# An encoder's first layer: norm factor r applied where the projections leave PSUM, raw X transposed

## The chip, the cores and the metric

The kernel runs on one core of a Trainium2 chip. The metric is the time of one launch on the device in microseconds (us). Beside it stand profiles: one execution recorded by the hardware profiler. PE is TensorE (its weight loads are a row PEld), DVE is VectorE, ACT is ScalarE, POOL is GpSimd, SP is SyncE, which issues most DMAs. Each engine works through its own instructions in order and waits on semaphores of the others.

## The reference, cut to what matters

A bidirectional encoder over 1024 tokens of width 1024, in float32, with two layers. Layer 0 mixes tokens by two-dimensional neighbourhood attention, layer 1 by grouped-query attention with rotary positions. The diff touches only layer 0's head:

```python
def rms_norm(x, g):
    y = xf * lax.rsqrt(jnp.mean(xf * xf, axis=-1, keepdims=True) + NORM_EPS)
    return (y * g.astype(jnp.float32)).astype(x.dtype)

h = rms_norm(x, norm_g[0])
q, k, v, gate = jnp.split(h @ w_in, 4, axis=-1)      # w_in: 1024 x 4096, 16 heads of 64
sc = einsum('bhqd,bhqnd->bhqn', q, k[window]) * scale + bias
o = einsum('bhqn,bhqnd->bhqd', softmax(sc), v[window])
y = (o * silu(gate)) @ w_out
```

The norm factor r = 1/sqrt(mean(x*x) + eps) is one number for each token; the gain g is one number for each of the 1024 features. So h @ w is r * ((x * g) @ w), row by row.

## The kernel before, in words

Tokens are handled in 8 tiles of 128. Every large matmul is made of three: both operands are split into a high part in the fp32r format and a low part, the remainder (split3, L302: high x high, high x low, low x high).

**The transposed input.** HTh and HTl hold the normalised, transposed input, high and low, for 8 tiles x 8 chunks of 128 features. to_ht (L420 to L427) makes them: PE transposes four 128x128 chunks into one PSUM bank (L425), ACT copies the bank into HTh (L426), DVE subtracts that copy from the bank into HTl (L427); two such halves make a tile.

**The weights.** The class Weights holds a queue of weight units. stage (L200) issues the DMA of a 512 KB unit from SP into one of a few slots; pump lets ACT make the high part wh (L215), and settle lets DVE make the low part wl (L216). A slot is free again when wl is done.

**The start of mixer_a (L697 to L786)** is a sequence written by hand. Per tile t: load X[t] (L706); square (L709, ACT's Square with a sum along the row); newton (L713 and L312 to L322: r by an integer first guess and three steps, 13 small DVE instructions on 1, 2 or 4 columns), which weave spreads between other pieces of work; scale (tiles 0, 1, 2, 4, 6: one DVE instruction X*r*g, L725; tiles 3, 5, 7: ACT times r, L727, then POOL times g, L728); then ht(t), the transposes of the scaled X. After that come vs[t][0] and vs[t][1], the two halves of the V projection of tile t for the first four heads (24 matmuls of 256 columns in all). Its result leaves PSUM by ACT into V's high part (L579) and by DVE into its low part (L580). PE's order is vs[t][0], transposes of tile t+1, vs[t][1].

**Beside it** SP loads the mask and the position bias (8 DMAs into U), expands U to U2 (16 DMAs, L778), and table (L618 to L627) loads a head's bias (L621) and subtracts it from the mask on POOL (L624).

**Then attention.** For head 0, qk_items runs the q and k projection: matmuls with 512 tokens as columns and 128 rows of features (64 of q, 64 of k). qk_evac (L583 to L609) copies the bank on ACT into a tile raw (L593), and from it ACT and DVE make the split q and k. gate_items (L516) does the same for the gate: ACT copies the bank to G (L520), ACT's tanh reads G (L521). For each head, scores (f_S), exponentials (f_E), transposes of the probabilities (f_T) and the product with V (f_AV) are interleaved with the projection of the following head and the gates, by a planner that fills PE's time by costs written beside each piece; V for the heads 4 to 15 is projected in the same way, through the same v_items.

PSUM's eight banks in this stage: pd (projections, 2), psS (scores, 2), psT (transposes, 2), psO (outputs, 2).

Of the kernel before, what the change touches and what calls it, by code (L numbers as in the profile page):

```python
# [11 lines left out]
F32 = mybir.dt.float32  # L12
# [3 lines left out]
AF = mybir.ActivationFunctionType  # L16
ALU = mybir.AluOpType
# [4 lines left out]
NT = 8  # L22
KC = 8
D = 1024
HD = 64
NH = 16
EPS = 1e-6
# [9 lines left out]
DT = (5, 2)  # L37
FIN = (4, 4)
HOLD = 2
DP = 1  # L40
KD, KS = 3, 4
QD = (2, 5, 8)
# [40 lines left out]
def lay_out(inp):  # L83
    g = {k: np.asarray(v) for k, v in inp.items()}
# [7 lines left out]
    aq, ak, av, ag = np.split(g["a_w_in"][0], 4, axis=1)  # L92
# [48 lines left out]
    def swap(v):  # L141
# [4 lines left out]
    return {  # L146
        "x": tokens(g["x"][0]), "wts": W, "rpb": rpb, "gains": gains, "hgains": hg,
        "mask": mask, "rope": np.stack([cosT, sinT], axis=1),
    }


@with_exitstack
def trunk(ctx, tc, x, wts, rpb, gains, hgains, mask, rope, out):
    nc = tc.nc
    sync, act, dve, pool, pe = nc.sync, nc.scalar, nc.vector, nc.gpsimd, nc.tensor

# [264 lines left out]
    def to_ht(pt, t, xn, cs=(0, 1)):  # L421
        for c in cs:
            ps = pt.tile([128, 4, 128], F32, name="t")
            for k in range(4):
                pe.transpose(ps[:, k], xn[:, (4 * c + k) * 128:(4 * c + k + 1) * 128], ident)  # L425
            act.activation(HTh[:, t, 4 * c:4 * c + 4], ps, AF.Copy)  # L426
            dve.tensor_tensor(HTl[:, t, 4 * c:4 * c + 4], ps, HTh[:, t, 4 * c:4 * c + 4], ALU.subtract)  # L427
# [124 lines left out]
    def mixer_a():  # L552
        with ExitStack() as es:
# [10 lines left out]
            def dalloc():  # L564
                return pd.tile([128, 512], F32, name="d")

            def valloc():
                return pd.tile([128, 512], F32, name="d")[:, :256]

            gg, ylive = {}, {}  # L570
# [3 lines left out]
            def v_items(qd, t):  # L574
                keys = [("av", qd, 0), ("av", qd, 1)]

                def evac(ps):
                    v = ps.rearrange("p (h d) -> p h d", h=4)
                    act.activation(V[:, t, :, 0:64], v, AF.Copy)  # L579
                    dve.tensor_tensor(V[:, t, :, 64:128], v, V[:, t, :, 0:64], ALU.subtract)  # L580
                return [d[0] for d in proj_N(keys, t, 256, valloc, evac, release=keys if t == NT - 1 else ())]

            def qk_evac(h, hf):  # L583
                def evac(ps):
                    if hf == 0:
                        QS[h] = qkp.tile([128, 1024], F32R, name="QS")
                        KA[h] = qkp.tile([128, 1024], F32R, name="KA")
                        KB[h] = qkp.tile([128, 1024], F32R, name="KB")
                    s = slice(hf * 512, (hf + 1) * 512)
                    lo, hi = slice(0, 64), slice(64, 128)  # L590
                    qs, ka, kb = QS[h], KA[h], KB[h]
                    raw = sb.tile([128, 512], F32, name="th", bufs=2)
                    act.activation(raw, ps, AF.Copy)  # L593
# [81 lines left out]
            def f_AV(h, kb):  # L675
# [3 lines left out]
                for hf in range(2):  # L679
# [12 lines left out]
                    if last:  # L692
                        fin = head_end(sb, h, hf, RS[h][:, 4 * hf:4 * hf + 4], OP[h][hf], ylive, 0, gg, talloc)
                        if fin:
                            later.add(FIN[0], fin)

            e2 = es.enter_context(ExitStack())  # L697
            ini = e2.enter_context(tc.tile_pool(name="ini", bufs=1))
            X = [ini.tile([128, D], F32, name=f"X{t}") for t in range(NT)]
            gt = ini.tile([128, D], F32, name="gain")  # L700
            junk = ini.tile([128, D], BF16, name="junk")
            stat = one.tile([128, 3, 8], F32, name="stat")
            wk = one.tile([128, 24], F32, name="wki")

            def load(t):
                sync.dma_start(X[t], x[t])  # L706

            def square(t):
                act.activation(junk, X[t], AF.Square, accum_out=stat[:, 0, t:t + 1])  # L709

            def newton(a, b):
                ms = stat[:, 1, a:b]
                return [lambda: dve.tensor_scalar(ms, stat[:, 0, a:b], 1.0 / D, EPS, op0=ALU.mult, op1=ALU.add)] \  # L713
                    + rsqrt_ops(stat[:, 2, a:b], ms, wk)

            def weave(ops, fs):
                per = -(-len(ops) // len(fs))
                for i, f in enumerate(fs):
                    for o in ops[i * per:(i + 1) * per]:
                        o()  # L720
                    f()

            def scale(t):
                if t % 2 == 0 or t == 1:
                    dve.scalar_tensor_tensor(X[t], X[t], stat[:, 2, t:t + 1], gt, op0=ALU.mult, op1=ALU.mult)  # L725
                else:
                    act.activation(X[t], X[t], AF.Copy, scale=stat[:, 2, t:t + 1])  # L727
                    pool.tensor_tensor(X[t], X[t], gt, ALU.mult)  # L728

            def ht(t):  # L730
                return [lambda c=c: to_ht(psT, t, X[t], (c,)) for c in range(2)]

            load(0)
            sync.dma_start(gt, bcast(gains, 0, D))
            load(1)
            WQ.stage(True)
            for t in range(2, NT):
                load(t)
            U = dram.tile([16, 8, 31, 24], F32, name="U")
            square(0)  # L740
            square(1)
            weave(newton(0, 1), [lambda: scale(0)])
            WQ.pump(True)
            WQ.pump(True)
            vs = [v_items(0, t) for t in range(NT)]
            weave(newton(1, 2), ht(0))
            scale(1)
            square(2)
            square(3)
            vs[0][0]()  # L750
            weave(newton(2, 4), ht(1))
            scale(2)
            scale(3)
            square(4)
            square(5)
            square(6)
            vs[0][1]()
            sync.dma_start(MK, mask)
            for c in range(8):
# [1 line left out]
            for t in range(1, NT):  # L761
                vs[t][0]()
                if t + 1 < NT:
                    weave(newton(4, 8) if t == 2 else [], ht(t + 1))
                if t == 1:
                    square(7)
                if t in (2, 3):
                    scale(2 * t)
                    scale(2 * t + 1)
                vs[t][1]()  # L770
                if t == 6:
                    table(0)
                WQ.pump(t > 2)
                if t == 3:
                    for r in range(16):
                        src = bass.AP(tensor=U.tensor, offset=U.offset + (15 - r) * 24,
                                      ap=[[5952, 16], [744, 8], [1, 384]])
                        sync.dma_start(U2[:, r * 8:(r + 1) * 8, :], src)  # L778
            e2.close()
            qkp = es.enter_context(tc.tile_pool(name="qkp", bufs=2))  # L780
            ptp = es.enter_context(tc.tile_pool(name="ptp", bufs=1))
# [22 lines left out]
            for h in range(NH):  # L804
# [24 lines left out]
                    dense += qk_items(h + 1)  # L829
                p = h // 2  # L830
                if h < 14:
                    dense += gate_items("ag", p, h % 2, dalloc, sb, gg)
                elif h == 14:
                    dense += gate_items("ag", 7, 0, dalloc, sb, gg) + gate_items("ag", 7, 1, dalloc, sb, gg)
# [454 lines left out]
    dense_phase(1)  # L1289


NAMES = ["x", "wts", "rpb", "gains", "hgains", "mask", "rope"]


# [13 lines left out]
```

## Time and profile before

| | before |
|---|---|
| median of 3 runs | 1585.03 us (1583.64 to 1585.88) |
| the profiled execution's own time | 1586.45 us |
| its span | 1584.7 us |
| mean granted clock of PE | 0.996 |
| busy share of the span: PE, DVE, ACT, POOL | 96%, 65%, 55%, 17% |

A timeline row reads: start in us, duration in us, engine, line of the kernel, operation, output<-inputs, their shapes, a count if several stand in the row, and in brackets how long the engine had been idle and what released it. A row of groups reads: line, engine, operation, names, shapes and count, then busy us in all and the mean ns of one, then the engine's idle time ahead of them and its releaser. A row of waits reads: who waited for whom, us in all, how often, the longest.

### The profile page before, as it was taken

What the parts mean: (1) busy time and instruction counts of PE and PEld (TensorE: products, weight loads), DVE (VectorE), ACT (ScalarE), POOL (GpSimd) and SP (SyncE); (2) the same over time, 40 slices, a digit from 0 to 9 for tenths busy, and PEclk for the clock granted to TensorE, in tenths of its full rate; (3) what the DMA queues carried; (4) which work ended last, traced back from release to release, by engine and by line L of the source; (5) the groups of instructions that cost most, each with busy time, mean ns of one, the idle gap of its engine ahead of it and who ended that gap; (6) DMA issues with size and microseconds to landing.
All of it is one profiled execution on the core that took longest, in us unless ns stands there. A gap on an engine that the chain in (4) does not pass through costs nothing.

```text
span 1584.7 us, 24269 instructions
## 1 busy us (share of the span) xinstructions
PE 1527.3 (96%) x9048; PEld 1331.9 (84%) x9048; DVE 1025.0 (65%) x2062; ACT 872.8 (55%) x1744; POOL 266.8 (17%) x372
## 2 busy tenths in 40 slices
PE   6999999999999999999999999999999999999997
PEld 5888988988988788888888889989888888778886
DVE  6566576476477436558867776777776877625636
ACT  6465465466376522334467766667666777622422
POOL 2102102102112010000212222433131200000023
PEclk9999999999999999999999999999999999999999
DMA  8211122132123971232210111102111213651113
GB/s 270 77 47 63 58 73 77 39 92 77 39 88 91 335 244 59 76 137 78 71 48 21 38 59 43 48 24 68 36 33 41 74 34 103 237 199 54 68 56 130
DMA packets 89861, 138.84 MB, mean 88 GB/s; under 512 B 16912, under 2 KB 55952, under 8 KB 89744
## 3 DMA queue, kind: packets, MB, share of 16 engines
q1 hardware_dynamic: 85136, 122.62, 23.6%
q10 hardware_dynamic: 4608, 14.68, 2.6%
q8 instruction: 71, 1.16, 0.3%
q14 instruction: 46, 0.38, 0.1%
HBM read 104.65 MB, written 36.15 MB: 89 GB/s over the span
## 4 chain that ended last, share of the span: by engine, by line
PE 39%; DVE 6%; ACT 5%; issue 2%; POOL 0%; ACTq 0%; DVEq 0%
PE d L300 21%; PE o L300 6%; PE s L300 6%; PE t L1063 5%; DVE PTl L1066 2%; ACT PTh L1065 1%; ACT P L1053 1%; DVE mn L1047 1%; DVE QS L1030 1%; PE t L425 1%; ACT QS L1029 1%; ACT wh L215 0%; ACT rb L508 0%; DVE wl L216 0%; ACT th L1025 0%
## 5 line engine op out<-in xcount | busy, mean ns | idle before, releaser
L300 PE MATMUL d<-wh,HTh 128*128 128x256 f32 (+1 forms) x1096 | 373.0, 340 | 4.9 <-ACT HTh L426 2.3
L300 PE MATMUL d<-wh,HTl 128*128 128x256 f32 (+1 forms) x1096 | 366.5, 334 | 1.5 <-DVE HTl L427 1.5
L300 PE MATMUL d<-wl,HTh 128*128 128x256 f32 (+1 forms) x1096 | 365.9, 334 | 0.0
L300 PEld LDWEIGHTS d<-wh,HTh 128*128 128x128 f32 x1096 | 208.3, 190 | 28.3 <-ACT HTh L426 2.8
L300 PEld LDWEIGHTS d<-wh,HTl 128*128 128x128 f32 x1096 | 208.1, 190 | 23.9 <-DVE HTl L427 2.2
L1066 DVE TENSOR_TENSOR PTl<-t,PTh 128x512 fp32r<-128x512 f32 x256 | 164.6, 684 | 96.0 <-ACT PTh L1065 95.3
L300 PEld LDWEIGHTS d<-wl,HTh 128*128 128x128 f32 x1096 | 208.5, 190 | 21.5
L300 PE MATMUL d<-HTh,wh 128*128 128x512 f32 x504 | 206.2, 409 | 0.0
L300 PE MATMUL d<-HTh,wl 128*128 128x512 f32 x504 | 198.2, 393 | 0.0
L300 PE MATMUL d<-HTl,wh 128*128 128x512 f32 x504 | 197.9, 393 | 0.0
L300 PE MATMUL o<-PTl,V 128*128 128x256 f32 (+2 forms) x672 | 174.9, 291 | 2.9 <-DVE PTl L1066 2.5
L300 PE MATMUL o<-PTh,V 128*128 128x256 f32 (+2 forms) x672 | 173.9, 289 | 1.2 <-ACT PTh L669 1.1
L1053 ACT ACTIVATE P<-s,mn 128x1024 f32<-128x1024 f32 x128 | 142.5, 1113 | 54.2 <-DVE mn L1047 54.0
L1065 ACT ACTIVATE PTh<-t 128x512 fp32r<-128x512 f32 x256 | 140.1, 593 | 54.3 <-PE t L1063 53.9
L1047 DVE TENSOR_REDUCE mn<-s 128x1 f32<-128x1024 f32 x128 | 154.9, 1210 | 10.8 <-PE s L300 10.4
L1063 PE MATMUL t<-ident,P 128*128 128x128 f32 x1024 | 137.4, 275 | 7.9 <-DVE PTl L1066 7.0
L300 PE MATMUL s<-KA,QS 128*128 128x512 f32 (+2 forms) x384 | 134.7, 405 | 10.0 <-ACT PTh L1065 5.6
L216 DVE TENSOR_TENSOR wl<-wstage,wh 128x1024 fp32r<-128x1024 f32 x89 | 114.1, 1288 | 41.1 <-ACT wh L215 40.6
L300 PEld LDWEIGHTS o<-PTl,V 128*128 128x128 f32 x672 | 129.1, 192 | 9.1 <-DVE PTl L1066 4.8
L1063 PEld LDWEIGHTS t<-ident,P 128*128 128x128 f32 x1024 | 114.8, 140 | 23.8 <-DVE PTl L1066 18.6
L300 PEld LDWEIGHTS o<-PTh,V 128*128 128x128 f32 x672 | 128.7, 192 | 5.5 <-ACT PTh L669 1.3
L300 PE MATMUL s<-KB,QS 128*128 128x512 f32 (+2 forms) x384 | 122.3, 373 | 0.0
(178 smaller groups left out, 2440.7 us busy)
## 6 DMA issues: line engine op xcount, KB each, us to landing
wstage<-in_wts SPq DMA_DIRECT2D x92, 512.0 KB
X<-in_x SPq DMA_DIRECT2D x16, 512.0 KB
pp<-ppD SPq DMA_DIRECT2D x32, 256.0 KB
rb<-rD SPq DMA_DIRECT2D x56, 128.0 KB
ppD<-th SPq DMA_DIRECT2D x24, 256.0 KB
xD<-X SPq DMA_DIRECT2D x8, 512.0 KB
X<-xD SPq DMA_DIRECT2D x8, 512.0 KB
yD0h<-rb SPq DMA_DIRECT2D x14, 256.0 KB
```

The lines of the kernel that those rows point to most:

```text
L216: self.rest = lambda: dve.tensor_tensor(lo, s, hi, ALU.subtract)
L300: pe.matmul(ps, a, b, start=first, stop=last, skip_group_check=True)
L425: pe.transpose(ps[:, k], xn[:, (4 * c + k) * 128:(4 * c + k + 1) * 128], ident)
L1029: act.activation(qs[own], raw[own], AF.Copy)
L1030: post.add(DQ, lambda qs=qs, own=own, oth=oth: dve.tensor_tensor(qs[oth], raw[own], qs[own], ALU.subtract))
L1047: dve.tensor_reduce(mn, ps, axis=AX.X, op=ALU.min)
L1053: act.activation(p, ps, AF.Exp, bias=mn, scale=-1.0, accum_out=RS[h, hf][:, t:t + 1])
L1063: pe.transpose(ps[:, i], p[:, k * 128:(k + 1) * 128], ident)
L1065: act.activation(PTh[:, ks, c], ps, AF.Copy)
L1066: dve.tensor_tensor(PTl[:, ks, c], ps, PTh[:, ks, c], ALU.subtract)
```

## The change

The norm's two factors are taken apart. g (per feature) goes in ahead of the projections, r (per token) where their results leave PSUM.

- **Tiles 0 and 1** (ht_k): the raw X is transposed; after the transpose the features lie on the partitions, so g is a column gT (128 x 8, a new input, loaded ahead of the weights). Each 128-column slice has an ACT instruction of its own (copy, scale g) and a DVE instruction of its own (bank * g - high part).
- **Tiles 2 to 7** (gained): POOL multiplies X by g into one of two buffers xg, and to_ht works on xg as before.
- **r** is worked out in pairs of tiles, newton(0, 2), (2, 4), (4, 6), (6, 8), each in one piece (the function weave goes). The squares stand behind the transposes.
- **V**: r is the scale of ACT's copy and of DVE's subtraction. valloc takes a bank of psO every second time while the start lasts.
- **q, k and gates**: they have tokens along the columns, so r is needed as a row, the same on all partitions. spread_r makes RB (128 x 1024), in two halves at t = 5 and 7: DVE copies r of a tile along 128 columns, PE transposes, ACT evicts. Then raw and G are made by DVE, bank * RB, in place of ACT's copy.
- **Order**: X0 comes in two halves ahead of gT and two weight units; X1 and the gain row behind them. 12 transposes of the identity (warm) stand at the head of PE's queue. The two splits of weights stand between the halves of tile 0.

```diff
+WARM = 12
-    def gate_items(key, pair, hf, alloc, sb, gg):
+    def gate_items(key, pair, hf, alloc, sb, gg, RB=None):
...
-            act.activation(G, ps, AF.Copy)
+            if RB is None:
+                act.activation(G, ps, AF.Copy)
+            else:
+                dve.tensor_tensor(G, ps, RB[:, hf * 512:(hf + 1) * 512], ALU.mult)
...
             def valloc():
+                early[1] += 1
+                if early[0] and early[1] % 2 == 0:
+                    return psO.tile([128, 512], F32, name="o")[:, :256]
                 return pd.tile([128, 512], F32, name="d")[:, :256]
...
-                    act.activation(V[:, t, :, 0:64], v, AF.Copy)
-                    dve.tensor_tensor(V[:, t, :, 64:128], v, V[:, t, :, 0:64], ALU.subtract)
+                    r = stat[:, 2, t:t + 1]
+                    act.activation(V[:, t, :, 0:64], v, AF.Copy, scale=r)
+                    dve.scalar_tensor_tensor(V[:, t, :, 64:128], v, r, V[:, t, :, 0:64], op0=ALU.mult, op1=ALU.subtract)
...
-                    act.activation(raw, ps, AF.Copy)
+                    dve.tensor_tensor(raw, ps, RB[:, s], ALU.mult)
...
+            def gained(t):
+                xg = ini.tile([128, D], F32, name="xg", bufs=2)
+                pool.tensor_tensor(xg, X[t], gt, ALU.mult)
+                return xg
+
+            def ht_k(t, c):
+                ps = psT.tile([128, 4, 128], F32, name="t")
+                for k in range(4):
+                    pe.transpose(ps[:, k], X[t][:, (4 * c + k) * 128:(4 * c + k + 1) * 128], ident)
+                for k in range(4):
+                    g, h = gT[:, 4 * c + k:4 * c + k + 1], HTh[:, t, 4 * c + k]
+                    act.activation(h, ps[:, k], AF.Copy, scale=g)
+                    dve.scalar_tensor_tensor(HTl[:, t, 4 * c + k], ps[:, k], g, h, op0=ALU.mult, op1=ALU.subtract)
+
+            def split():
+                WQ.pump(True)
+                WQ.settle()
+
+            def warm():
+                ps = psS.tile([128, 512], F32, name="s").rearrange("p (a c) -> p a c", a=4)
+                for k in range(WARM):
+                    pe.transpose(ps[:, k % 4], ident, ident)
+
+            def spread_r(hf):
+                ps = psT.tile([128, 4, 128], F32, name="t")
+                for t in range(4):
+                    i = 4 * hf + t
+                    rw = sb.tile([128, 128], F32, name="sp", bufs=3)
+                    dve.tensor_copy(rw, stat[:, 2, i:i + 1].to_broadcast([128, 128]))
+                    pe.transpose(ps[:, t], rw, ident)
+                act.activation(RB[:, hf * 512:(hf + 1) * 512], ps.rearrange("p t c -> p (t c)"), AF.Copy)
+
+            for c in (slice(0, 512), slice(512, 1024)):
+                sync.dma_start(X[0][:, c], x[0][:, c])
+            sync.dma_start(gT, gain0)
+            WQ.stage(True)
+            load(1)
             sync.dma_start(gt, bcast(gains, 0, D))
...
+            warm()
+            ht_k(0, 0)
+            split()
+            ht_k(0, 1)
+            split()
+            vs[0][0]()
+            ht_k(1, 0)
             square(0)
+            ht_k(1, 1)
             square(1)
...
+            xg = gained(2)
+            newton(0, 2)
             vs[0][1]()
...
             for t in range(1, NT):
                 vs[t][0]()
                 if t + 1 < NT:
-                    weave(newton(4, 8) if t == 2 else [], ht(t + 1))
...
+                    to_ht(psT, t + 1, xg)
+                    square(t + 1)
+                    if t % 2 == 0:
+                        newton(t, t + 2)
+                if t + 2 < NT:
+                    xg = gained(t + 2)
+                if t in (5, 7):
+                    spread_r(t // 6)
                 vs[t][1]()
```

More of the change, by code (lines that the diff above doesn't have):

```diff
@@ L148, in lay_out, with trunk @@
         "mask": mask, "rope": np.stack([cosT, sinT], axis=1),
+        "gain0": gains[0].reshape(8, 128).T,
     }
 @with_exitstack
-def trunk(ctx, tc, x, wts, rpb, gains, hgains, mask, rope, out):
+def trunk(ctx, tc, x, wts, rpb, gains, hgains, mask, rope, gain0, out):
     nc = tc.nc
@@ L695, in f_AV @@
                             later.add(FIN[0], fin)
+            stat = one.tile([128, 3, 8], F32, name="stat")
+            wk = one.tile([128, 24], F32, name="wki")
+            RB = one.tile([128, 1024], F32, name="RB")
             e2 = es.enter_context(ExitStack())
@@ L700, in mixer_a @@
             gt = ini.tile([128, D], F32, name="gain")
+            gT = ini.tile([128, 8], F32, name="gT")
             junk = ini.tile([128, D], BF16, name="junk")
-            stat = one.tile([128, 3, 8], F32, name="stat")
-            wk = one.tile([128, 24], F32, name="wki")
             def load(t):
@@ L712, in newton @@
                 ms = stat[:, 1, a:b]
[L713 to L728, printed above, removed]
@@ L730, in ht @@
-            def ht(t):
-                return [lambda c=c: to_ht(psT, t, X[t], (c,)) for c in range(2)]
-            load(0)
+                dve.tensor_scalar(ms, stat[:, 0, a:b], 1.0 / D, EPS, op0=ALU.mult, op1=ALU.add)
+                rsqrt(stat[:, 2, a:b], ms, wk)
+            def gained(t):
[10 more added lines that the diff above has]
+                    dve.scalar_tensor_tensor(HTl[:, t, 4 * c + k], ps[:, k], g, h, op0=ALU.mult, op1=ALU.subtract)
@@ L734, in mixer_a @@
+            U = dram.tile([16, 8, 31, 24], F32, name="U")
+            for c in (slice(0, 512), slice(512, 1024)):
[3 more added lines that the diff above has]
+            load(1)
             sync.dma_start(gt, bcast(gains, 0, D))
-            load(1)
-            WQ.stage(True)
             for t in range(2, NT):
                 load(t)
-            U = dram.tile([16, 8, 31, 24], F32, name="U")
+            vs = [v_items(0, t) for t in range(NT)]
@@ L740, in mixer_a @@
+            warm()
[5 more added lines that the diff above has]
+            ht_k(1, 0)
             square(0)
+            ht_k(1, 1)
             square(1)
[L742 to L756, printed above, removed]
+            xg = gained(2)
+            newton(0, 2)
             vs[0][1]()
@@ L763, in mixer_a @@
                 if t + 1 < NT:
-                    weave(newton(4, 8) if t == 2 else [], ht(t + 1))
[L765 to L769, printed above, removed]
+                    to_ht(psT, t + 1, xg)
[6 more added lines that the diff above has]
+                    spread_r(t // 6)
                 vs[t][1]()
@@ L1289, in trunk @@
     dense_phase(1)
-NAMES = ["x", "wts", "rpb", "gains", "hgains", "mask", "rope"]
+NAMES = ["x", "wts", "rpb", "gains", "hgains", "mask", "rope", "gain0"]
 def kernel(**inputs):
```

6 lines of the change are left out of this document (4 added, 2 removed).

## The prediction

> **What bounds the kernel now.** I read the page's totals first, then the busy time by stage, then what TensorE (PE) waits for in the stage that the diff touches.
>
> ```profile
> span 1584.7 us, 24269 instructions
> ...
> PE 1527.3 (96%) x9048; PEld 1331.9 (84%) x9048; DVE 1025.0 (65%) x2062; ACT 872.8 (55%) x1744; POOL 266.8 (17%) x372
> ```
>
> PE is busy for 96% of the span, so time can be won only in its gaps, and whatever opens a new gap is paid in full. By stage (columns: PE, weight load, VectorE = DVE, ScalarE = ACT, GpSimd = POOL, granted clock, DMA share, GB/s):
>
> ```profile
> 0.00:50.00 50.00, 35.48 (x258) 33.57 (x259) 32.06 (x78) 28.39 (x48) 11.49 (x14) 1.00 0.74 239
> 50.00:620.00 570.00, 561.82 (x3097) 485.30 (x3096) 340.27 (x744) 308.90 (x674) 83.08 (x107) 1.00 0.30 97
> ```
>
> In the first 50 us, where layer 0's input is normalised and transposed and the first V projection runs, PE is idle for 14.5 us. In the following 570 us of layer 0 it is idle for 8.2 us in all. Two more rows say what the 14.5 consist of and where the stage ends, at the first q/k matmul:
>
> ```profile
> PE t L425 <- DVE X L725: 10.7, 4, 8.8
> PE d L300 <- ACT HTh L426: 2.3, 2, 1.2
> PE d L300 <- DVE HTl L427: 1.5, 2, 1.3
> ```
> ```profile
> 49.71 0.40 PE L300 MATMUL d<-HTh,wh 128*128 128x512 f32 x1
> ```
>
> The waits for the scaled X (10.7 us, 8.8 of them before the first transpose) are what the change can remove: it transposes X as it comes. The stage's end at 49.71 is my clock: I work out when the first q/k matmul starts afterwards, and pass the difference on to the end, since behind it PE has almost no slack to absorb a delay.
>
> **The change part by part.** *Prices.* Rows of ACT, DVE, and POOL in the first 50 us (busy, then mean ns of one):
>
> ```profile
> L426 ACT ACTIVATE HTh<-t 128x512 fp32r<-128x512 f32 x16 | 8.8, 594 | 8.5 <-PE t L425 8.5
> L709 ACT ACTIVATE junk<-X 128x1024 bf16<-128x1024 f32 x8 | 8.4, 1056 | 4.7 <-DMA X<-in_x 4.6
> ...
> L727 ACT ACTIVATE X<-X,stat 128x1024 f32<-128x1024 f32 x3 | 3.5, 1152 | 2.5 <-DVE stat L322 2.5
> L579 ACT ACTIVATE V<-d 128x256 fp32r<-128x256 f32 x8 | 3.0, 379 | 4.8 <-PE d L300 4.8
> L709 ACT ACTIVATION_READ_ACCUMULATOR junk<-X 128x1 f32 x8 | 1.5, 191 | 0.0
> ```
> ```profile
> L427 DVE TENSOR_TENSOR HTl<-t,HTh 128x512 fp32r<-128x512 f32 x16 | 10.5, 684 | 3.4 <-ACT HTh L426 3.3
> ...
> L725 DVE SCALAR_TENSOR_TENSOR X<-X,stat,gain 128x1024 f32<-128x1024 f32 x5 | 6.4, 1278 | 0.0
> L580 DVE TENSOR_TENSOR V<-d,V 128x256 fp32r<-128x256 f32 x7 | 2.9, 421 | 4.4 <-ACT V L579 4.4
> L728 POOL TENSOR_TENSOR X<-X,gain 128x1024 f32<-128x1024 f32 x3 | 8.7, 2884 | 27.8 <-ACT X L727 27.8
> ```
> ```profile
> 0.72 1.28 ACT L709 ACT_TABLE_LOAD   x1 [0.72 <-PEq L1300]
> 4.18 1.06 ACT L709 ACTIVATE junk<-X 128x1024 bf16<-128x1024 f32 x1 [2.18 <-DMA X<-in_x]
> ...
> 9.01 1.06 ACT L215 ACTIVATE wh<-wstage 128x1024 fp32r<-128x1024 f32 x1
> ...
> 19.39 1.15 ACT L727 ACTIVATE X<-X,stat 128x1024 f32<-128x1024 f32 x1 [1.23 <-DVE stat L322]
> ...
> 24.11 1.07 ACT L426 ACTIVATE HTh<-t 128x512 fp32r<-128x512 f32 x2
> ```
> ```profile
> 10.10 1.22 DVE L216 TENSOR_TENSOR wl<-wstage,wh 128x1024 fp32r<-128x1024 f32 x1 [1.47 <-ACT wh L215]
> ...
> 16.49 0.16 DVE L713 TENSOR_SCALAR stat<-stat 128x2 f32<-128x2 f32 x1
> ...
> 19.13 0.16 DVE L322 SCALAR_TENSOR_TENSOR stat<-wki 128x2 f32<-128x2 f32 x1
> ```
>
> *Tiles 0 and 1: 16 slices of 128 columns.* No row shows a 128-column eviction with a scale by pointer. ACT: 256 columns 0.379, 512 columns 0.594, so 0.27 for 128 on the same line, and 0.10 for the pointer (L727's 1.152 against L215's 1.06): 0.37. DVE likewise: 0.684 and 0.421 give 0.29, and L725 against the wl row (1.28 against 1.22) adds 0.06: 0.35. Each low slice needs its high slice, and in the changed program ACT's next high slice waits for DVE's last low one, so the two engines alternate. Handing over costs 0.03 one way (wh ends at 10.07, wl starts at 10.10) and about 0.07 back (stat ends at 19.29, L727 starts at 19.39). One pair: 0.37 + 0.03 + 0.35 + 0.07 = **0.82**. Bounds: 0.37, if they overlapped, and 1.28, two evictions at the 512-column prices; I stay with 0.82, as the interpolation has rows on one side only by a factor of two.
>
> *Start.* ACT's first instruction waits for the gain column gT, which stands behind X0 in SP's queue; X0 released ACT at 4.18, so gT about 4.5 (an estimate). The activation table load (1.28) now stands behind that wait and not ahead of X0, as at 0.72 before: first slice at 5.8. (Bounds 4.5 and 7.)
>
> *Head.* 16 pairs from 5.8: 13.1. Twice a weight split stands between blocks of four pairs: ACT is free 0.45 before DVE ends its block; 1.06 + 0.03 + 1.22, less this 0.45 and less the next block's first ACT slice, which lies beside wl (0.48 with hand-over): 1.4 each. One square between the blocks of tile 1 costs 1.25 (1.056 + 0.191) less 0.45: 0.8. The blocks end at 5.8 + 13.1 + 2.8 + 0.8 = 22.5, the second square at 23.3. Now r for tiles 0 and 1: the same 13 small operations took 2.80 (16.49 to 19.29) with one 0.6 eviction between them, so 2.2, to 25.5. V(0)'s eviction needs r, and in ACT's order HTh(2) stands behind V(0).
>
> *Holds by POOL.* Six multiplies replace three. What DVE does beside one, by these rows:
>
> ```profile
> 34.59 3.16 POOL L728 TENSOR_TENSOR X<-X,gain 128x1024 f32<-128x1024 f32 x1 [0.77 <-ACT X L727]
> ```
> ```profile
> 35.76 3.07 DVE L216 TENSOR_TENSOR wl<-wstage,wh 128x1024 fp32r<-128x1024 f32 x1
> ```
> ```profile
> 1021.20 0.76 POOL L888 TENSOR_TENSOR qt<-qt,tab 128x256 f32<-128x256 f32 x1
> ...
> 1021.38 0.60 DVE L322 SCALAR_TENSOR_TENSOR wk<-wk 128x8 f32<-128x8 f32 x1
> ```
>
> The wl of 1.22 took 3.07, ending 1.08 after POOL's end; a small operation of the same rsqrt line took 0.60, to POOL's end, instead of 0.16. So I let such an operation wait until the multiply ends. The third multiply starts when the transposes of tile 2 free its buffer, near 23.2, and ends near 25.95; r then ends at 27.95 instead of 25.5 (hold 2.5), V(0) follows, and HTh(2) starts at **28.3**, against 24.11 before: 4.2 late.
>
> *Tiles 2 to 7.* Two prices of PE:
>
> ```profile
> 26.77 1.04 PE L425 MATMUL t<-ident,X 128*128 128x128 f32 x8
> 27.57 0.36 PE L300 MATMUL d<-wh,HTh 128*128 128x256 f32 x1
> ...
> 30.40 0.28 PE L300 MATMUL d<-wh,HTl 128*128 128x256 f32 x1
> ```
>
> Transposes of a tile take 0.8 up to the next matmul, and the 24 matmuls 2.9: 3.7 per tile if PE leads. ACT and DVE lead instead, since each second V(t) waits for square(t+1) and a new r. HTh(2) to HTh(4): two tiles of HTh (1.2 each), two squares (1.25 each), V(1) and V(2) (0.4 each), r 2.2, holds 3.6 (multiplies of tiles 5 and 6 fall on it), hand-overs 0.35: 11.85 against 7.4, so HTh(4) at 40.15. HTh(4) to HTh(6): two tiles 2.4, squares 2.5, V(3) and V(4) 0.8, the weight split wh 1.06, r 2.2, a hold of 0.9, 0.7 of hand-overs: 10.55, HTh(6) at 50.7.
>
> *The two spreads.* RB needs r in a row: four DVE copies, four transposes, one ACT eviction, and PE's queue has these transposes ahead of the second half of V(5) and V(7). Behind HTh(6) stands wl and HTl(6) to 53.2, then copies and transposes, an estimate of 1.4: 54.6. Behind HTl(5) (46.0) stand only vs(5)'s first half (1.43) and tile 6's transposes (0.8), done at 48.2; the first copy reaches PE near 54.1: PE waits for 5.9 us. Then vs(5)'s second half, vs(6) with tile 7's transposes, vs(7)'s first half (1.43 each, as 12 of the 24): 61.2. The last r comes at 62.4, V(6) at 63.3, second spread 64.6 (PE idle 2.7), last half 66.0. First q/k matmul: 66.0 - 49.71 = **+16.3**.
>
> *The clock.* Laid beside this chain, PE's queue has new gaps of 4.8 (ahead of vs(2)), 3.9 (vs(4)), 5.9, 2.4 (vs(6)) and 2.7. What followed a gap of 2.59 in this run:
>
> ```profile
> 789.77 1.22 PE L300 MATMUL s<-KA,QS 128*128 128x512 f32 x2 [2.59 <-DVE QS L1030]
> ```
> ```profile
> 789.45:792.85 3.40, 3.08 (x7) 2.49 (x8) 3.30 (x7) 0.47 (x1) 0.00 (x0) 0.50 0.06 12
> 792.90:796.00 3.10, 3.10 (x15) 2.54 (x14) 2.94 (x10) 0.35 (x1) 0.00 (x0) 1.00 0.42 153
> ```
>
> Half clock for 3.4 us, which costs 1.7 where PE leads. After the first two gaps ACT leads (0.3 each), after the 5.9 and the last one PE does: 2 x 1.7 + 0.6 = **+4.0**. Bounds: 0 and 5 x 1.7 = 8.5. The Trainium skill ("TensorE: Matmul & The Clock Gate", HAM oscillation) sets the limit at idle gaps over about 3.4 us. By it the 2.7 gap would leave the clock alone, and the sum would be 1.7 lower; the row above shows half clock after 2.59, so I keep the row.
>
> *The rest of layer 0.* 48 evictions of 128x512 (32 raw q/k, 16 gates) go from ACT to DVE with RB as second operand:
>
> ```profile
> L593 ACT ACTIVATE th<-d x32: 577/597/599, 55.4 to 496.6; 128x512 f32<-128x512 f32 x32
> ```
>
> DVE gains 48 x 0.69 = 33 (340 becomes 373 of 570), ACT loses 48 x 0.60 = 29. Both keep a third of the stage free; I take **0**, bounds -2 (some of the 8.2 idle goes) and +10 (PE waits a further 0.2 at each). The 12 warming transposes run before X lands: 0. The bias table's DMAs stand in SP's queue behind weight loads that now wait for later wl's; POOL already waits for them, long before attention needs the table:
>
> ```profile
> 45.62 2.16 POOL L624 TENSOR_TENSOR tb<-MK,u 128x128 f32<-128x128 f32 x5 [7.86 <-DMA u<-U]
> ```
>
> Cost 0, as the q/k matmuls of head 0 lie between; without that cover it would be bounded by about another 8.
>
> *Sum.* 16.3 + 4.0 = +20.3. The profiled execution took 1586.45 (span 1584.7), 1.42 over the median of the runs; 1586.45 + 20.3 = 1606.7, and in terms of the median 1605.3. I write **1605**.
>
> One rule speaks to the slices: the Trainium skill ("VectorE: DVE Perf Modes", the section on the TRN2 errata) gives each instruction a fixed cost and advises tiles of 512 elements or more. From its cycle table I estimate 0.25 on ACT and 0.26 on DVE for 128 columns, a pair of 0.61 with hand-overs, and 16 x 0.21 = 3.4 less: 1602. No row here shows the size; the sum keeps 0.82.
>
> **The rivals.**
> *Faster: the slices overlap and nothing holds r.* If ACT runs ahead of DVE (0.37 per pair, 16 x 0.45 = 7.2 less) and the 7.0 of holds vanish, PE leads again; it then waits for the two spreads (5.9 + 2.7 = 8.6) instead of for L725 (10.7): -2.1, 1583. It decides when the added waits fall below 10.7. For it: X needs no r before its transposes. Against it: the order of the semaphores.
> *No holds.* Small operations of 2 to 8 elements may slip past POOL (the 0.60 row is one case): 16.3 - 7.0 = 9.3, and half of the last window's clock loss goes with the shorter gaps, leaving 2.5: +11.8, 1597.
> *The clock stays up.* The gaps hold some matmuls or the warming helps: +16.3, 1601.
> *The clock falls after every gap.* 16.3 + 8.5 = +24.8, 1610.
> *Attention loses too.* DVE is late for its evictions, 48 x 0.2 = 10 on top: 1615. Against it: DVE was idle for 40% of that stage.
> *The change doesn't do what it says:* the norm still gates V through r, so taking it off the transposes gains nothing; that is in the forecast's chain already.
>
> **How the numbers follow.** Forecast 0.40, no holds 0.20, clock stays 0.17, clock falls 0.13, attention 0.05, faster rival 0.05. The range must leave out no more than 0.2: the two 0.05 cases lie outside. Its low end is the no-holds case with the clock staying up and a pair cheaper by 0.15 (1585 + 9.3 - 2.4 = 1592); its high end is the clock-falls case and 2 for the start's late bound: 1612. A measurement of this kernel can tell 0.2%, 3.2 us, from no change: faster 0.04, same 0.03, slower 0.93.
>
> **What would show each step.** First high slice near 5.8 and pairs 0.82 apart; HTh(2) near 28.3 and HTh(4) near 40; small rsqrt operations of 0.5 to 2.7 where POOL multiplies; PE waits of some 6 and 3 us at the spread's transposes, both put down to DVE; the first q/k matmul near 66 plus the clock's share; a clock of 0.5 behind the gaps; 50 us later PE's idle time unchanged at about 8 per 570. The forecast is wrong if the pairs start 0.4 apart, if r comes in 2.2 beside a running multiply, or if q/k starts before 60.

## The result and the profile after

The changed kernel takes 1611.26 us (median of 4 runs, 1609.78 to 1612.44) against 1584.34 for the kernel before (4 runs): a ratio of 1.0173, 95% interval 1.0156 to 1.019, 27 us slower. The forecast was 1605, with a range from 1592 to 1612, so the measured time lies 0.7 inside its upper end. The profiled execution took 1610.51, so the traces lie 24.0 apart and the medians 27: of that difference 2.1 is the profile of before, which lies above its median, and 0.8 the profile after, which lies below its own.

The page's totals and the stages after (the first 74 us, then the 570 us behind them, to be read against the first 50 us and the 570 behind them before):

```profile
span 1608.7 us, 24458 instructions
...
PE 1540.2 (96%) x9068; PEld 1341.0 (83%) x9068; DVE 1056.8 (66%) x2131; ACT 850.3 (53%) x1707; POOL 276.6 (17%) x375
```
```profile
0.00:74.00 74.00, 50.36 (x287) 46.85 (x288) 38.46 (x101) 31.86 (x61) 18.07 (x17) 0.86 0.51 162
74.00:644.00 570.00, 559.35 (x3080) 481.73 (x3079) 364.98 (x789) 282.14 (x623) 85.25 (x107) 1.00 0.30 97
```

In the start PE is busy for 15 us longer than before, with 29 instructions more (granted clock 0.86), and is idle for 23.6 us (before: 14.5). In the 570 us behind it PE is idle for 10.7 us (before: 8.2). The first q/k matmul and what PE waited for in the start:

```profile
71.57 0.46 PE L302 MATMUL d<-HTh,wh 128*128 128x512 f32 x1
```
```profile
PE t L758 <- DVE sp L757: 7.2, 2, 4.6
PE d L302 <- ACT HTh L428: 5.4, 2, 2.8
PE d L302 <- ACT wh L217: 4.9, 1, 4.9
PE t L427 <- DVE HTl L741: 2.8, 1, 2.8
```

The waits for X are gone, as the change means them to be. In their place stand the spreads (7.2), HTh held by r (5.4), the first weight split behind the slices (4.9) and the slices of tile 1 (2.8).

The attention stage shows in the 32 evictions of raw q/k (count, shortest, median and longest in ns, first and last start):

```profile
L604 DVE TENSOR_TENSOR th<-d,RB x32: 675/691/693, 77.3 to 522.6; 128x512 f32<-128x512 f32 x32
```

Before, they ran from 55.4 to 496.6. The first is 21.9 late, the last 26.0: attention adds 4.1. The rest of the span gives back 2.0, which is the 24.0; apart from the last few us of each, the profile of before has two stretches of half clock there, at 789 and 1383, and the one after has one, at 816.

**The slices, the table, the holds.** The first two pairs, on ACT and on DVE:

```profile
5.73 1.28 ACT L740 ACT_TABLE_LOAD   x1 [5.73 <-DMA gT<-in_gain]
7.03 0.37 ACT L740 ACTIVATE HTh<-t,gT 128x128 fp32r<-128x128 f32 x1
7.81 0.37 ACT L740 ACTIVATE HTh<-t,gT 128x128 fp32r<-128x128 f32 x1 [0.42 <-DVE HTl L741]
```
```profile
7.43 0.35 DVE L741 SCALAR_TENSOR_TENSOR HTl<-t,gT,HTh 128x128 fp32r<-128x128 f32 x1 [7.43 <-ACT HTh L740]
```

Pairs are 0.78 apart (7.03 to 7.81), and gT came at 5.73. That moment scatters: in the profiles of e1 and e3 below, whose head is the same, gT came at 4.52 and the first slice at 5.82.

```profile
5.82 0.37 ACT L740 ACTIVATE HTh<-t,gT 128x128 fp32r<-128x128 f32 x1
```

Beside POOL's multiplies DVE looks like this:

```profile
13.96 5.71 POOL L731 TENSOR_TENSOR xg<-X,gain 128x1024 f32<-128x1024 f32 x2 [12.68 <-DMA X<-in_x]
24.89 2.37 POOL L731 TENSOR_TENSOR xg<-X,gain 128x1024 f32<-128x1024 f32 x1 [5.22 <-PE t L427]
...
38.45 2.37 POOL L731 TENSOR_TENSOR xg<-X,gain 128x1024 f32<-128x1024 f32 x1 [1.33 <-DMA U<-U]
```
```profile
15.17 2.25 DVE L218 TENSOR_TENSOR wl<-wstage,wh 128x1024 fp32r<-128x1024 f32 x1 [0.59 <-ACT wh L217]
...
24.98 2.29 DVE L322 TENSOR_TENSOR wki<-wki 128x2 f32<-128x2 f32 x1
27.31 0.16 DVE L323 TENSOR_TENSOR wki<-wki 128x2 f32<-128x2 f32 x1
...
38.56 2.28 DVE L324 SCALAR_TENSOR_TENSOR wki<-wki 128x2 f32<-128x2 f32 x1
```

An instruction on two elements a partition takes 2.29 in place of 0.16 and ends when POOL's multiply ends (27.27 and 27.26). What ACT then has to wait for:

```profile
28.93 0.47 ACT L590 ACTIVATE V<-d,stat 128x256 fp32r<-128x256 f32 x1 [4.59 <-DVE stat L324]
29.31 1.08 ACT L428 ACTIVATE HTh<-t 128x512 fp32r<-128x512 f32 x2
...
41.52 0.47 ACT L590 ACTIVATE V<-d,stat 128x256 fp32r<-128x256 f32 x1 [5.28 <-DVE stat L324]
41.89 1.08 ACT L428 ACTIVATE HTh<-t 128x512 fp32r<-128x512 f32 x2
...
51.41 0.47 ACT L590 ACTIVATE V<-d,stat 128x256 fp32r<-128x256 f32 x1 [3.15 <-DVE stat L324]
```

V(0), V(2) and V(4) wait for r, and HTh(2), HTh(4) and HTh(6) stand behind them in ACT's queue. The clock in five stretches of the same trace:

```profile
24.00:27.30 3.30, 3.30 (x16) 3.02 (x14) 2.83 (x5) 0.34 (x2) 2.37 (x1) 0.50 0.79 174
30.80:34.00 3.20, 3.20 (x15) 3.20 (x16) 0.90 (x2) 0.98 (x3) 0.00 (x0) 0.50 0.94 264
45.00:47.60 2.60, 2.60 (x14) 2.60 (x13) 2.17 (x3) 1.88 (x4) 0.87 (x1) 0.50 0.05 8
55.00:61.50 6.50, 5.93 (x27) 5.67 (x28) 1.40 (x6) 1.07 (x2) 2.13 (x5) 0.50 0.33 113
68.60:71.80 3.20, 3.20 (x16) 3.07 (x15) 0.08 (x1) 0.60 (x1) 0.00 (x0) 0.52 0.00 0
```

I call some 3.4 us of half clock a window. The fourth stretch is two windows long: six windows behind five waits of PE of 2.6 to 4.7 us (they end at 23.75, 29.95, 42.53, 55.57 and 68.11).

### The profile page after: what moved, and what is told of

Its sections match the earlier page's. It is cut to its first block, busy times and chain, and to the rows that moved or that the text cites. A ratio compares the mean times of both kernels' runs of the same rounds, so it can differ in the third digit from the quotient of the medians.

```text
span 1608.7 us, 24458 instructions
## 1 busy us (share of the span) xinstructions
PE 1540.2 (96%) x9068; PEld 1341.0 (83%) x9068; DVE 1056.8 (66%) x2131; ACT 850.3 (53%) x1707; POOL 276.6 (17%) x375
## 4 chain that ended last, share of the span: by engine, by line
PE 38%; DVE 6%; ACT 5%; issue 2%; POOL 0%; ACTq 0%; DVEq 0%
PE d L302 21%; PE o L302 6%; PE s L302 5%; PE t L1092 5%; DVE PTl L1095 2%; ACT PTh L1094 1%; ACT P L1082 1%; DVE mn L1076 1%; DVE QS L1059 1%; PE t L427 1%; ACT QS L1058 0%; ACT wh L217 0%; ACT rb L510 0%; DVE wl L218 0%; ACT th L1054 0%
## 5 line engine op out<-in xcount | busy, mean ns | idle before, releaser
L302 PE MATMUL d<-wh,HTh 128*128 128x256 f32 (+1 forms) x1064 | 364.6, 343 | 13.4 <-ACT HTh L428 5.4
L302 PE MATMUL d<-wl,HTh 128*128 128x256 f32 (+1 forms) x1064 | 357.5, 336 | 1.5 <-DVE wl L218 1.5
L302 PE MATMUL d<-wh,HTl 128*128 128x256 f32 (+1 forms) x1064 | 357.8, 336 | 0.4 <-DVE HTl L429 0.4
L302 PEld LDWEIGHTS d<-wh,HTh 128*128 128x128 f32 x1064 | 203.1, 191 | 37.4 <-ACT HTh L428 5.9
L302 PEld LDWEIGHTS d<-wl,HTh 128*128 128x128 f32 x1064 | 203.1, 191 | 23.6 <-DVE wl L218 2.1
L302 PEld LDWEIGHTS d<-wh,HTl 128*128 128x128 f32 x1064 | 202.9, 191 | 22.6 <-DVE HTl L429 0.9
L1076 DVE TENSOR_REDUCE mn<-s 128x1 f32<-128x1024 f32 x128 | 154.7, 1209 | 10.7 <-PE s L302 10.3
L302 PEld LDWEIGHTS o<-PTl,V 128*128 128x128 f32 x672 | 127.9, 190 | 10.7 <-DVE PTl L1095 4.1
```

The costliest lines, as they stand in the source:

```text
L302: pe.matmul(ps, a, b, start=first, stop=last, skip_group_check=True)
L1076: dve.tensor_reduce(mn, ps, axis=AX.X, op=ALU.min)
```

## The experiments

My theory: the start loses by a chain (slices, r ahead of V, POOL's holds, spreads) and by the clock behind its gaps, and passes its lateness on; what attention loses was open. The rival in most runs: the part named lies beside something else and costs little. Each ratio is to the kernel before, timed beside the run. Differences from the changed kernel compare medians of different sessions, in which the kernel before moved by 1.4 us (1582.97 to 1584.34).

**Spreads later** (e1), on the changed kernel:

```diff
-                if t in (5, 7):
-                    spread_r(t // 6)
...
-            for d in qk_items(0):
+            for i, d in enumerate(qk_items(0)):
+                if i == 1:
+                    spread_r(0)
+                    spread_r(1)
```

> Both spreads of r moved behind the last V matmuls, between the first two pieces of head 0's q/k projection; all else as in the changed kernel (1611.3, first q/k matmul at 71.57). My theory (each spread holds PE until r is there, 4.65 + 2.59 us, and both gaps are followed by half clock, three windows of 3.4 us): these waits go, a wait of 1 to 3 us for HTh of tile 6 and V stays, the first q/k matmul comes near 63, the time is 1603 to 1605, ratio to before 1.012 to 1.013. Rival (the spreads only stand where PE would have waited for HTh and V anyway): at most 2 us less, 1609 or more, ratio 1.016.

Measured: 1607.79, ratio 1.0151 (1.0136 to 1.0167), 3.5 below the changed kernel. The first q/k matmul did come 9.2 earlier, yet PE stopped a few matmuls later:

```profile
62.32 0.40 PE L302 MATMUL d<-HTh,wh 128*128 128x512 f32 x1
...
65.83 1.73 PE L758 MATMUL t<-ident,sp 128*128 128x128 f32 x8 [1.97 <-DVE sp L757]
```

The copies stood behind a wl in DVE's queue; PE was idle for 1.97, and the clock fell again, so that the first eviction came only 3.9 earlier. Of the 9.2, a part stands ahead of the edit, as gT landed 1.2 earlier in this profile. Neither theory is borne out in full: the wait moved.

**No multiplies** (e2): `gained(t)` returns X[t], which leaves the gain out for tiles 2 to 7.

> Tiles 2 to 7 are transposed without the gain: this leaves out the multiplication by g for these tiles, so POOL has none of its six multiplies; all else as in the changed kernel. My theory (POOL's multiplies hold DVE's small operations and a wl on the path: 1.03 + 2.13 + 0.70 + 2.12 + 0.69 = 6.7 us over the changed kernel's first 50): no DVE operation of the rsqrt is longer than 0.25, first q/k matmul near 65, time 1604 to 1606, ratio 1.013. Rival (what is held lies beside PE's or ACT's work): at most 2 less, 1609 or more, ratio 1.016.

Measured: 1602.82, ratio 1.012 (1.0106 to 1.0134): 8.4 less, first q/k matmul 8.0 earlier:

```profile
63.61 0.52 PE L302 MATMUL d<-HTh,wh 128*128 128x512 f32 x1
```

The holds are on the path, and a little more than their own 6.7 goes with them (up to 0.5 of it is gT, which landed at 5.22 here).

**Gaps filled** (e3): `fill(n)` puts n transposes of the identity into PE's queue.

```diff
+                if t in (2, 4):
+                    fill(20)
                 vs[t][0]()
+                if t == 1:
+                    fill(20)
...
                 if t in (5, 7):
+                    fill(36 if t == 5 else 18)
                     spread_r(t // 6)
```

> Transposes of the identity into spare banks stand in PE's queue ahead of the five instructions at which PE waits for 2.6 to 4.7 us (20, 20, 20, 36 and 18 of them), so that PE is not idle; all else as in the changed kernel. My theory (idle stretches from 2.6 us on bring half clock, six windows of 3.4 us in the changed kernel's first 74 us, of which those where PE leads cost 1.7 each): at most one or two such windows are left, the first q/k matmul comes 5 to 7 us earlier, time 1604 to 1606, ratio 1.013. Rival (the clock's loss lies beside the wait for r): within 2 of the changed kernel, ratio 1.016 or more.

Measured: 1607.09, ratio 1.0146 (1.013 to 1.0161), 4.2 less; first q/k matmul at 68.61, 3.0 earlier. From 18 us on three windows of half clock are in its trace in place of six, behind waits of 2.20, 1.40 and 1.79 that the fills had not covered. So three windows fewer went with 3 to 4 us, but the intervals of the two ratios leave a wide margin, and gT landed 1.2 earlier in this profile. The clock's price isn't settled by this run.

**The evictions alone** (e4), on the kernel before:

```diff
-                    act.activation(raw, ps, AF.Copy)
+                    dve.tensor_tensor(raw, ps, RB[:, s], ALU.mult)
...
+            pool.memset(RB, 1.0)
```

and the same for G.

> The kernel before with one part of the change alone: the 48 evictions of raw q/k and gates are made by DVE as a product with RB, filled with ones once, in place of ACT's copy. By the traces, what follows the first q/k matmul took 1537.1 after the change and 1535.0 before, so my theory gives +2.1: 1586.4, ratio 1.0013. Rival one (hidden, as I costed it): 0. Rival two (each eviction late by 0.2): +10, ratio 1.006.

Measured: 1591.36, ratio 1.0045 (1.0032 to 1.0057): 7 us (5.1 to 9.0), nearest to rival two. In its profile, which lies 1.8 below that median, the last eviction is 4.9 late. What PE waited for from 50 to 620, before and in this run:

```profile
PE t L666 <- ACT sp L658: 5.8, 9, 1.4
```
```profile
PE t L669 <- ACT sp L661: 8.7, 17, 1.6
PE o L300 <- DVE PTl L673: 1.1, 4, 0.3
```

Before, ACT's exponentials (sp) made PE wait 9 times for 5.8 in all, now 17 times for 8.7. The queues show why for nine of the 17, waits of 0.22 to 0.31 and 2.3 in all:

```profile
193.45 3.46 DVE L216 TENSOR_TENSOR wl<-wstage,wh 128x1024 fp32r<-128x1024 f32 x2
196.83 0.68 DVE L596 TENSOR_TENSOR th<-d,RB 128x512 f32<-128x512 f32 x1
```
```profile
197.54 0.63 ACT L599 ACTIVATE QS<-th 64x512 fp32r<-64x512 f32 x1 [2.43 <-DVE th L596]
...
199.37 0.62 ACT L661 ACTIVATE sp<-sp,mn 128x384 f32<-128x384 f32 x1
```
```profile
200.13 0.55 PE L669 MATMUL t<-ident,sp 128*128 128x128 f32 x3 [0.31 <-ACT sp L661]
```

Here the raw tile (th) waits in DVE's queue behind two weight splits. ACT, which made it itself before the change, waits for it with the split q (QS) at the head of its queue, and the exponential stands behind that. Each of the nine waits has such a QS some 2.6 us ahead of it; in the kernel before, no wait of PE for an exponential has one. The rest of the 7 us is not traced.

**Warming the kernel before** (e5): `warm(34)` at the head of PE's queue, nothing else.

> The kernel before with 34 transposes of the identity at the head of PE's queue, from 1.3 to about 9 us, and nothing else of the change. In the kernel before PE works at half clock until 18.0. My theory (an idle PE brings half clock, in the start as elsewhere): the first transposes and V matmuls run at full clock, the first q/k matmul comes 1 to 3 us earlier than 49.7, time 1581 to 1583, ratio 0.998 to 0.999. Rival (in that stretch PE waits for X and HTh anyway): no difference, ratio 1.000.

Measured: 1582.07, ratio 0.9993 (0.9984 to 1.0002): no difference shown, though the interval holds the theory's 0.999 too. The first eight transposes of X run at full pace (1.09 us, 1.94 before), but PE then waits for 1.92, and the V matmuls behind that are 0.21 apart again:

```profile
8.89 1.09 PE L425 MATMUL t<-ident,X 128*128 128x128 f32 x8 [1.36 <-DVE X L725]
...
13.10 0.41 PE L300 MATMUL d<-wh,HTh 128*128 128x256 f32 x1
13.32 0.41 PE L300 MATMUL d<-wl,HTh 128*128 128x256 f32 x1
```

Full pace is back by 17, about 1 us earlier than before. The first q/k matmul starts at 49.73:

```profile
49.73 0.40 PE L300 MATMUL d<-HTh,wh 128*128 128x512 f32 x1
```

In this trace the rival holds: what PE gained it waits for at the next tile (1.41 for X at 21.25, before 0.56). It is no test of a start at full clock throughout.

**The head mended** (e6):

```diff
+            act.activation(tl, ident[:, 0:1], AF.Copy)
+            sync.dma_start(gT, gain0)
...
                 for k in range(4):
                     act.activation(HTh[:, t, 4 * c + k], ps[:, k], AF.Copy, scale=gT[...])
+                for k in range(4):
                     dve.scalar_tensor_tensor(HTl[:, t, 4 * c + k], ps[:, k], gT[...], HTh[...], ...)
```

> The changed kernel with its head alone mended: gT is loaded ahead of X0, a one-column copy brings the activation table in while X0 is loaded, and each half tile's four high slices are issued ahead of its four low ones, so that ACT and DVE do not alternate. Theory one (the first 23.7 us of slices, table and splits are on the path 1:1): the slices of tile 1 end 5 to 7 us earlier (3 by the table and gT, the rest by the alternation of 0.42 each), V(0) 4 to 6 earlier, time about 1606, ratio 1.014. Rival (r sets the time: the newton of tiles 0 and 1 runs into POOL's first two multiplies, 14 to 19.7, and the same holds come later): 2 us or less, 1609, ratio 1.016.

Measured: 1605.72, ratio 1.0139 (1.0122 to 1.0155), 5.5 less, first q/k matmul at 64.41. Theory one holds: the head is on the path. Which of its three edits (gT first, the table early, no alternation) gains how much, this run doesn't tell.

**r earlier** (e7): square 0 ahead of the first slice, square 1 behind the second split, newton(0, 2) ahead of tile 1's second half; then

```diff
-                    square(t + 1)
-                    if t % 2 == 0:
-                        newton(t, t + 2)
+                    if t + 3 < NT:
+                        square(t + 3)
+                    if t % 2 == 1:
+                        newton(t + 1, t + 3)
```

> The changed kernel with the squares and the newtons moved earlier, so that r of a pair is worked out one to two tiles ahead of its V eviction (square 0 ahead of the first slice, square 1 behind the second split, squares 2 and 3 behind tile 1's slices, square t+3 at tile t). Theory one (V(t)'s wait for r in ACT's queue, with HTh of the following tiles behind it, makes the middle of the start long; ACT waited 4.6 + 5.3 + 3.2 + 2.5 us for r): most of these 15 us go, PE waits only at the spreads, the first q/k matmul comes 8 to 10 us earlier, 1601 to 1603, ratio 1.011. Rival (POOL's multiplies and the spreads are the limit whatever the order of r): 3 us or less, 1608, ratio 1.015.

Measured: 1604.11, ratio 1.0132 (1.0117 to 1.0147), 7.2 less, first q/k matmul at 65.06, 6.5 earlier. The time lies between the two, nearer to theory one.

**All edits of the start** (e8): e6, e7 and the spreads ahead of the third and fifth piece of the q/k projection.

> Both edits of the two runs ahead of this one, and the spreads behind the first pieces of head 0's q/k projection (the first half of RB in the middle of the first 512 tokens' matmuls, the second half at the second's begin). If what I named is the whole loss of the start, PE leads there: the first q/k matmul comes at 46 to 49, as before the change or earlier, and what is left over is the attention stage's loss of 4 to 7 us by DVE's evictions: 1585 to 1591, ratio 1.001 to 1.004. If something else holds the start (the six multiplies' holds, the weights), 1595 or more, ratio 1.007.

Measured: 1601.42, ratio 1.0117 (1.0101 to 1.0134). The first q/k matmul is where it was before the change, and the second spread then stops PE for 4.1 us, in the middle of the projection:

```profile
49.67 0.40 PE L302 MATMUL d<-HTh,wh 128*128 128x512 f32 x1
...
61.82 1.24 PE L760 MATMUL t<-ident,sp 128*128 128x128 f32 x4 [4.13 <-DVE sp L759]
```

The copies waited in DVE's queue behind the first raw tile's work, and half clock followed again: the first eviction is 2.4 late, the fifth 9.0. The mark came where the first case had it and the time where the second had it: the lateness had moved behind the mark.

**Spreads where r is ready** (f1): as e8, but `if t in (6, 7): spread_r(t - 6)` ahead of V's second half.

> As the run with all edits of the start, but the two spreads stand ahead of the second halves of V(6) and V(7), where r of all tiles has been ready since tile 5, and not between the pieces of the q/k projection. In that run the first q/k matmul came at 49.67, as before the change, yet the fifth eviction was 9.0 late: PE waited 5.5 us for the copies of the spreads, and half clock followed. Theory one (the copies stood behind evictions and weight splits in DVE's queue; here they do not): q/k starts at 50 to 52, the fifth eviction is 1.5 to 3 late, and 4 to 7 are left for the attention stage: 1589 to 1593, ratio 1.003 to 1.006. Rival (the spreads cost the same wherever they stand): 1598 or more, ratio 1.009.

Measured: 1598.74, ratio 1.0097 (1.0081 to 1.0112), with f2 the best that keeps r behind the projections. The first q/k matmul is at 55.33, and from 17 us on its gaps are:

```profile
21.11 1.12 PE L427 MATMUL t<-ident,xg 128*128 128x128 f32 x4 [3.57 <-DVE HTl L742]
39.73 0.39 PE L302 MATMUL o<-wh,HTl 128*128 128x256 f32 x1 [3.63 <-DVE HTl L429]
47.69 1.61 PE L760 MATMUL t<-ident,sp 128*128 128x128 f32 x4 [1.89 <-DVE sp L759]
```

The rival's time is nearer than mine, but the trace doesn't bear out its reason: the first two gaps, 7.2 of 9.1 us, are not the spreads' but DVE's, small operations held by multiplies (2.15 at 15.70, 2.29 at 34.67) with HTl behind them in the queue.

**One copy to ACT** (f2, on f1), `act.activation(kb[lo, s], kb[hi, s], AF.Copy)` for `dve.tensor_copy`:

> The run above with one more edit: the copy of kb's low part to the lower 64 partitions (64x512, 0.42 us on DVE, 32 times) goes from DVE to ACT, which lost 48 evictions. Theory (the attention stage loses because DVE's queue is longer, so that the score reductions come late): 2 to 4 us off the run above. Rival (what counts is the order ACT after DVE after PE for each raw tile): no gain, or a loss as the copy takes about 0.63 on ACT.

Measured: 1598.7, ratio 1.0098 (1.0082 to 1.0114): no gain.

**Raw q/k alone** (f3) and **all evictions with that copy on ACT** (f4), both on the kernel before:

> The kernel before with the 32 evictions of raw q/k alone on DVE (product with ones); the 16 gate evictions stay on ACT. All 48 cost 7 (ratio 1.0045). If each costs the same: 4.7, ratio 1.003. If the raw tiles alone count, because split q and k and then the scores follow them: 7, ratio 1.0045. If the gates alone count, by the tanh and head ends that follow them: 0 to 1, ratio 1.000.

Measured: 1588.09, ratio 1.0029 (1.0019 to 1.0038), 4.6 us, or 0.14 for each eviction, as for all 48. The intervals leave room for the raw tiles to make up anything from a third of the loss to all of it; that the gates alone count is excluded.

> All 48 evictions on DVE (product with ones) on the kernel before, and the 32 copies of kb's low part from DVE to ACT: DVE's load in the attention stage is then 33 - 13 = 20 us above the kernel before. Theory (DVE's load makes the score reductions late): half of the 7 us goes, ratio 1.002. Rival (each eviction's own lateness): 7 as before, ratio 1.0045.

Measured: 1590.08, ratio 1.0043 (1.003 to 1.0055): nothing comes back. From 50 to 620 DVE's busy time falls from 362 to 347 us (340 in the kernel before), and ACT's rises from 282 to 300 (309 before), so both are near their old loads, and PE still waits 17 times for the exponentials, 9.4 in all. So it isn't the load of either engine as a whole. That each eviction hands its work on later fits, and e4's rows show how for a part of it; how the whole of the 7 us comes about stays open.

No version of the change beats the kernel before.

## Why the prediction was right, and where it was short

- **Where it landed.** The direction and the path through the start came out as forecast, the size a third larger (27 against 20). That 1611 still lies inside the range is partly luck: the upper end was built from the clock's worst case and a late start, while what carried the time there was attention, which the range left out.
- **The bound and the pass-through.** Right: PE is busy for 96% in both, and e2 (8.0 earlier at the first q/k matmul, 8.4 less in all) shows it. e1 and e8 show its limit: a wait moved behind the mark isn't saved.
- **Pairs 0.82.** Measured 0.78, with ACT and DVE alternating as read from the program. By the table of the Trainium skill ("VectorE: DVE Perf Modes", TRN2 errata) I had estimated 0.61; the trace shows 0.37 on ACT and 0.35 on DVE, as interpolated from the rows.
- **Start 5.8.** In the changed kernel's profile gT landed at 5.73, not 4.5, so the first slice came at 7.03. With the same head, e1 and e3 have 4.52 and 5.82, as forecast: the 1.2 is scatter of one execution, not a wrong step. e6 shows that the head was on the path: 5.5 us.
- **Holds.** Right in kind and place: 2.1 at tile 0's r, 2.1 and 0.7 at tile 2's, 0.7 at tile 4's. Missed: the second wl took 2.25 in place of 1.22, though the prediction shows such a row. The rival without holds falls by the rows above and by e2.
- **HTh(2) 28.3, HTh(4) 40.15, HTh(6) 50.7.** Measured 29.31, 41.89, 52.73, so 1.0, 1.7 and 2.0 late. gT (1.2) and the held wl (1.0) would cover that; this is a sum and not a run.
- **Spreads 5.9 and 2.7.** Measured 4.65 and 2.59.
- **The clock, +4.0 in a sum of 20.3.** The first q/k matmul was due at 70.0 and came at 71.57; with the clock up it would have been 66.0, by the rival of 8.5 it would have been 74.5. From the first spread's transposes to this mark the chain without clock had 11.9, the trace has 16.0 (55.57 to 71.57). The 4.1 between them hold three windows of half clock where the forecast charged two, 3.4. So the term was near in size. Its gaps were not all as drawn: those ahead of vs(2) and vs(4) were 2.6 and 2.8, not 4.8 and 3.9; none came ahead of vs(6); and one of 2.8 ahead of tile 2's second half had not been seen. No run isolates the term. The Trainium skill's limit ("TensorE: Matmul & The Clock Gate", HAM oscillation: gaps over about 3.4 us) doesn't agree with this case: half clock followed 2.59 here and 1.89 in f1, but not f1's 3.63.
- **The rest of layer 0 at 0.** This is the step that failed. I took DVE's idle 40% for cover. But a moved eviction waits its turn in DVE's queue, and ACT's next work waits for it: e4 shows 7 us (5.1 to 9.0), the changed kernel's own trace 4.1, with PE idle for 10.7 in place of 8.2. The bound of +10 and the attention rival had it, at a chance of 0.05. With 21.9 for the start and some 4 to 7 here, the 27 of the medians is accounted for to within what single executions scatter.
- **The warming transposes at 0.** Right: the first V matmuls ran 0.21 apart, as before. 34 transposes (e5) lifted the pace for the first transposes of X, and no gain is shown.

## What to carry to other kernels

A factor that is moved behind a matmul doesn't leave the path if an eviction that needs it stands, in the same engine's queue, ahead of the operands of the next matmul: follow each queue in order and ask what is behind the one that waits. Where PE is busy for 96%, moving an eviction to an engine with idle time isn't free: 48 moved evictions cost 7 us here, and lightening that engine gave nothing back. Ask what the eviction queues behind on its new engine, and what its old engine then waits for. And a gap on PE can cost more than its length: half clock followed most gaps of 1.9 us and more here, though not all.

## What the runs showed of the hardware that was not expected

The column of the granted clock does not always show the slow start. In the changed kernel's profile it reads 1.00 throughout the first 20 us, while matmuls of one form are 0.21 apart at first and 0.12 later (in e1, e2 and e3 the same stretch reads 0.50 from 8 to 10 us on):

```profile
12.81 0.41 PE L302 MATMUL d<-wl,HTh 128*128 128x256 f32 x1
13.03 0.41 PE L302 MATMUL d<-wh,HTl 128*128 128x256 f32 x1
...
17.82 0.28 PE L302 MATMUL d<-wh,HTh 128*128 128x256 f32 x1
17.93 0.28 PE L302 MATMUL d<-wl,HTh 128*128 128x256 f32 x1
```

Behind the twelve warming transposes (2.8 us of PE) the eight of X still took 1.91 here; behind 34 (6.2 us, e5) they took 1.09, but a wait of 1.92 later the matmuls were 0.21 apart again.

Nor does the length of a gap alone decide whether half clock follows. It followed gaps of 1.9 to 2.0 us (f1 at 47.69, e1 at 65.83), shorter than the 2.59 that I had taken as the smallest. It did not follow a gap of 1.96 in the changed kernel (at 151.51), nor the longest of f1, 3.63 at 39.73, though it did follow the same gap of 3.63 in f2 (at 39.15). f1 behind its second and third gap:

```profile
39.70:43.10 3.40, 3.37 (x29) 3.38 (x30) 2.90 (x5) 1.09 (x2) 0.00 (x0) 1.00 0.51 163
48.20:51.50 3.30, 3.24 (x15) 2.86 (x15) 0.57 (x2) 0.60 (x1) 0.91 (x3) 0.50 0.00 0
```

Behind the second gap the matmuls are 0.12 apart, so there the column is right. What decides stays open.
